# A two-layer hybrid decoder step: gate projections dealt out between the convolutions, squares and convolution states on ScalarE, second weight parts on VectorE

## Chip, cores and metric

One core of one Trainium2 chip runs the whole program. The metric is the device time of one execution in microseconds (us), as the median of several runs. The engines are named as the profile names them: PE is TensorE's matmul, PEld its weight load, DVE VectorE, ACT ScalarE, POOL GpSimd, SP SyncE (which here only issues transfers).

## What is computed

Each of two layers takes 320 tokens (256 of a prompt, 8 x 8 of samples) through one wide input projection and three token mixers, and merges them by gates:

```python
x = x + (sum_b sigmoid(h_gate_b) * (branch_b @ w_br_b)) @ w_out     # b: pooling, latent attention, DeltaNet
xn = rmsnorm(x);  h = xn @ w_in      # 7344 columns: pooling, q, kv, z's, q/k/v of DeltaNet, gates (3 x 1024)
# DeltaNet branch: a causal convolution of width 4 on 1536 channels, silu, l2-norm of q and k,
# then a chunked delta rule (chunks of 64 tokens); the last 3 pre-convolution rows are an output
qkv = silu(y);  y[t] = sum_j xx[t + j] * w[j];  conv_state = xx[-3:]
q_d, k_d = l2norm(q), l2norm(k)
```

## The kernel before

**Projections.** Activations stand transposed: 128 channels on the partitions, 320 tokens along the row. Every 128 columns of a weight are one projection: SP loads 512 KB into one of four buffers `wraw` (L176), `split_w` makes two parts of it, `wh` by ACT (L196) and the remainder `wl = wraw - wh` (L197), and `mm3` multiplies by 24 matmuls of 320 columns (8 slices times `wh`·`xnH`, `wh`·`xnL`, `wl`·`xnH`: L220, L221, L222) into a PSUM tile. `wh` and `wl` are double buffered, as is the PSUM tile `pj`. The remainder is made by DVE, except where the number of the split within the layer stands in the list `lo` of the layer's table `KS`: there POOL makes it.

**A gate** (`gate`, L460, L461) is such a projection, an elementwise product on DVE and a tanh on ACT. Each layer has 24 of them, and they depend on nothing but the normalised input, so they can stand anywhere before the merge.

**A convolution** (`conv`, `conv_out`) is a projection, two products with `rn` into `V` (L496, L497), the state columns in and out of `V` on POOL (L498 in; L499, L500 out into `cnew`), a first tap on ACT (L503), three taps on DVE (L505), a tanh on ACT (L507) and two products on DVE (L512, L516). There are twelve a layer: four for k (`unit(0, p)`, tile `kk`), four for q (`unit(1, p)`, tile `qq`), four for v (`value`, tile `co`). For k and q a square `sq` follows on POOL (L538), a matmul that sums it (L540) and, when all four are there, a logarithm and an exponential over them (`unit_norm`, L545, L546).

**Order.** The scheduler of the framework sets each engine's order by a timeline of its own, from the order in which the code is written; every engine then runs its instructions in order. The table `KS` holds one row of numbers a layer. `fillers` is a list of closures (the remaining convolutions, pooling, late projections), in the order `fo`; `fill(n)` writes out the next n. `kk`, `ft`, `fu`, `fy`, `fz` say how many fillers go between which steps of the DeltaNet preparation and recurrence; `ga`, `gm`, `gb`, `gs` how many gates are written after the decay products, within the triangular inverse, ahead of the q products, and within the recurrence over chunks.

**Stages of a layer.** The convolution stage ends with the first matmul `Y` (L793): it holds the convolutions, the decay products `D`, `AT` and the 8 x 8 inverse `R` (L756 to L768), a chain of small DVE steps. After it come the rest of the triangular inverse, the chunk products, the recurrence (L1041 `ws`, L1048 `us`, L1056 the new state) and the attention queries, then attention, then the merge.

Of the kernel before, what the change touches and what calls it, by code (L numbers as in the profile page):

```python
# [14 lines left out]
AF = mybir.ActivationFunctionType  # L15
# [22 lines left out]
WARM, WN, TA = 8, 6, 1  # L38
XK, XL, XD = 2, 2, (0, 2, 4)

KS = [{'kk': [1, 1, 2, 3], 'ga': 3, 'gm': [0, 2, 0], 'un': 16, 'gb': 0, 'gc': [0, 0, 0], 'ft': [5, 2, 3, 3, 2], 'fu': [0, 1, 2, 1], 'fn': 3, 'gs': [0, 0, 2, 1, 0], 'gq': 0, 'gp': [0, 0, 0, 0, 0, 1, 1, 0], 'ge': [1, 1, 1], 'ya': 'B', 'zb': 'A', 'fy': [2, 1, 1], 'fz': [1, 1, 1], 'p1': [2, 2, 2, 2], 'p2': [2, 2, 2, 2], 'hd': [3, 0, 2, 1, 1, 1, 0, 0], 'fo': [0, 1, 2, 3, 4, 5, 6, 7, 8, 9, 12, 13, 10, 14, 11, 18, 15, 16, 17, 19], 'to': [0, 2, 6, 1, 3, 5, 7, 13, 14, 8, 15, 16, 18, 9, 17, 10, 4, 11, 12], 'bt': ['A', 'A', 'A', 'A', 'M'], 'lo': [1, 2, 4, 5, 8, 13], 'zp': [-1, -1, -1, 19, -1, -1, -1, -1], 'f8': 3}, {'kk': [1, 1, 2, 3], 'ga': 3, 'gm': [0, 0, 0], 'un': 8, 'gb': 1, 'gc': [0, 0, 0], 'ft': [5, 2, 3, 3, 1], 'fu': [0, 1, 2, 1], 'fn': 3, 'gs': [0, 0, 2, 1, 0], 'gq': 0, 'gp': [0, 0, 0, 0, 0, 1, 1, 0], 'ge': [1, 1, 2], 'ya': 'B', 'zb': 'B', 'fy': [2, 1, 2], 'fz': [1, 0, 1], 'p1': [2, 2, 3, 1], 'p2': [2, 2, 2, 2], 'hd': [3, 0, 2, 1, 1, 1, 0, 0], 'fo': [0, 1, 5, 2, 3, 4, 6, 7, 8, 9, 12, 13, 10, 14, 11, 18, 15, 16, 17, 19], 'to': [0, 2, 5, 1, 6, 3, 7, 13, 14, 8, 15, 16, 18, 9, 17, 10, 4, 11, 12], 'bt': ['A', 'A', 'A', 'M', 'M'], 'lo': [1, 2, 4, 5, 15], 'zp': [-1, -1, -1, 19, -1, -1, -1, -1], 'f8': 3}]
LEVELS = (8, 16, 32)

GP, GL, SPILL = (1, 5), (2, 2, 2, 2, 2, 2, 1, 1), 14
# [72 lines left out]
def trunk(tc, I, O, layers=2):  # L117
    nc = tc.nc
    ctx = ExitStack()
    mult, add, sub, amax, amin = ALU.mult, ALU.add, ALU.subtract, ALU.max, ALU.min  # L120
# [18 lines left out]
    def ps(tag, name):  # L139
        return banks["pool"].tile([128, 512], F32, tag=tag, name=name, bufs=banks["n"][tag])  # L140
# [23 lines left out]
    act = nc.scalar.activation  # L164
# [182 lines left out]
    for t, (x, n) in enumerate(xnat):  # L347
        sq = pt.tile([128, 4 * T], F32, tag="l2", name="sq", bufs=2)[:, :DM]
# [19 lines left out]
    for k in range(8):  # L368
        b = ps(tags[k % len(tags)], "xt")
# [14 lines left out]
    b = ps(RNB, "rn")  # L384
# [25 lines left out]
    for l in range(layers):  # L410
        turn[0], K = 0, KS[l]
        P = prm[l]
# [62 lines left out]
        b = ps(STB, "stT")  # L475
# [6 lines left out]
        cnew = pt.tile([128, 12, 32], F32, name="cnew")  # L482
# [3 lines left out]
        b = ps("A", "spT")  # L486
# [80 lines left out]
        i = act(SM[32:40, :], SM[32:40, :], AF.Exp, scale=-1.0)  # L567
# [12 lines left out]
        gc = SM[64:72, :]  # L580
# [13 lines left out]
        b = ps("M", "tok")  # L594
# [8 lines left out]
        b = ps("M", "el")  # L603
# [77 lines left out]
        fillers = [lambda p=p: unit(1, p) for p in range(4)]  # L681
# [99 lines left out]
        for m in LEVELS:  # L781
            last = m == LEVELS[-1]
            Ys = []
            for t in range(2):
# [10 lines left out]
                for hi in second if last else (slice(0, 128),):  # L795
                    i = act(Yb[hi], Y[hi], AF.Copy)
# [4 lines left out]
            for t in range(2):  # L801
# [11 lines left out]
                else:  # L813
                    o = first(TS_[:, 0], m)
# [15 lines left out]
        for q in range(3):  # L830
            b = ps("pj", "cn")
# [38 lines left out]
        p2 = p2c.enter_context(tc.tile_pool(name=f"p2_{l}", bufs=1, side="right", reuse_waits="tile"))  # L870
# [213 lines left out]
        sq = kv5[:, :, 0]  # L1084
# [7 lines left out]
        for p in range(4):  # L1092
            b = ps("A", "oT")
# [15 lines left out]
        for p in range(4):  # L1109
            b = ps("A", "kn")  # L1110
# [222 lines left out]
        with tc.manual_schedule(engines={mybir.EngineType.PE, mybir.EngineType.DVE, mybir.EngineType.Activation, mybir.EngineType.Pool}):  # L1333
# [9 lines left out]
            for t in range(2):  # L1343
                b = ps("A", "vv")
# [7 lines left out]
            for h in range(11):  # L1352
# [10 lines left out]
                if h in GP:  # L1363
                    b = gate_mm("A", w)
# [12 lines left out]
            gs = [gate_w() for _ in range(GL[0])]  # L1377
# [3 lines left out]
            o = None  # L1381
            for bb in range(NB):
# [18 lines left out]
                if two:  # L1401
                    b = gate_mm("A", gs[1][1], ks=(0, 4))
# [25 lines left out]
        b = ps("A", "oml")  # L1428
# [33 lines left out]
        for mp in range(4):  # L1462
            for i in range(2):
                m = 2 * mp + i
                w = split_w(load_w(I["w_out"][l][:, m * 128 : m * 128 + 128], 8, 128), 8)
                b = ps("pj", "wo")
# [3 lines left out]
                if not last:  # L1470
                    i = split_x(xn[0][:, m, :], xn[1][:, m, :], xT[:, m, :], scale=prm[l + 1][:, m : m + 1])
# [57 lines left out]
```

## Time and profile before

| | before |
|---|---|
| median of 3 runs | 1063.83 us (1061.71 to 1064.25) |
| the profiled execution's own time | 1066.27 us |
| its span in the trace | 1064.5 us |
| PE busy in the span | 995.7 us (94%) |
| DVE busy | 725.8 us (68%) |
| ACT busy | 456.5 us (43%) |
| POOL busy | 338.0 us (32%) |

The difference of 1.8 us between the execution's time and the span is what lies around the first and the last profiled instruction. Busy shares are means over stages; the rows below are by stage.

### The profile page before, as it was taken

Reading aid. Unit: us, or ns where it says so; the run is one execution under the profiler, and the core shown is the slowest. Engines: PE = TensorE matmul, PEld = TensorE weight load, DVE = VectorE, ACT = ScalarE, POOL = GpSimd, SP = SyncE. Lnnn points to the kernel's source line nnn. Section 1 sums busy time; section 2 is a strip of 40 time slices with the busy share of each in tenths; the row PEclk is TensorE's granted clock in tenths of the full one; section 3 lists DMA queues with packets and bytes.
Section 4 is the critical chain, followed back from the end, with each engine's and each line's share of the span. In section 5 each row is a group of like instructions: output and inputs, shape, how many; then the busy total and the mean of one; then the engine's idle time right before and its main releaser. Section 6 shows DMA issues by size and latency. Waiting matters only on the chain.

```text
span 1064.5 us, 24733 instructions
## 1 busy us (share of the span) xinstructions
PE 995.7 (94%) x10179; PEld 866.4 (81%) x10179; DVE 725.8 (68%) x1387; ACT 456.5 (43%) x810; POOL 338.0 (32%) x469
## 2 busy tenths in 40 slices
PE   8988899999979999989989979999998899999996
PEld 6877798987857888779978868999876678777996
DVE  3999884558676666558748988656666657574872
ACT  5663353543433333334545624336344333334453
POOL 3666221215151101025445542211335211100641
PEclk8999899999989999999998989999998899999998
DMA  8532333733645776258663332355255376742961
GB/s 231 155 97 80 100 92 84 206 95 106 190 139 158 237 242 222 96 154 233 158 200 79 101 99 70 101 153 141 71 162 182 102 254 211 248 157 83 278 169 50
DMA packets 202697, 159.22 MB, mean 150 GB/s; under 512 B 27704, under 2 KB 191826, under 8 KB 200010
## 3 DMA queue, kind: packets, MB, share of 16 engines
q1 hardware_dynamic: 176364, 98.47, 34.1%
q0 software_dynamic: 7424, 48.75, 13.0%
q10 hardware_dynamic: 18798, 10.44, 3.4%
q8 instruction: 80, 1.31, 0.5%
q14 instruction: 31, 0.25, 0.1%
HBM read 144.17 MB, written 13.68 MB: 148 GB/s over the span
## 4 chain that ended last, share of the span: by engine, by line
PE 71%; DVE 15%; ACT 5%; issue 3%; DMA 3%; POOL 1%; ACTq 0%; SPq 0%; DVEq 0%; POOLq 0%
PE sc L1166 6%; PE pv L1237 5%; PE gate L220 5%; PE pj L220 5%; PE pj L222 5%; PE gate L222 4%; PE pj L221 4%; PE gate L221 4%; DVE cy L505 4%; PE br L220 3%; PE br L221 2%; DVE wl L197 2%; PE br L222 2%; PE wo L220 2%; PE wo L222 2%
## 5 line engine op out<-in xcount | busy, mean ns | idle before, releaser
L196 ACT ACTIVATE wh<-wraw 128x1024 fp32r<-128x1024 f32 (+1 forms) x180 | 166.4, 935 | 174.3 <-PE pj L221 93.0
L197 DVE TENSOR_TENSOR wl<-wraw,wh 128x1024 fp32r<-128x1024 f32 (+2 forms) x165 | 187.9, 1147 | 69.2 <-ACT wh L196 68.2
L220 PE MATMUL pj<-xnH,wh 128*128 128x320 f32 (+1 forms) x528 | 174.7, 331 | 13.5 <-DVE V L497 7.6
L222 PE MATMUL pj<-xnH,wl 128*128 128x320 f32 (+1 forms) x528 | 172.3, 326 | 6.7 <-DVE wl L197 6.4
L221 PE MATMUL pj<-xnL,wh 128*128 128x320 f32 (+1 forms) x528 | 170.0, 322 | 0.0
L220 PE MATMUL gate<-xnH,wh 128*128 128x320 f32 x384 | 124.7, 325 | 1.5 <-DVE V L497 1.5
L222 PE MATMUL gate<-xnH,wl 128*128 128x320 f32 x384 | 120.5, 314 | 1.8 <-DVE wl L197 1.3
L220 PEld LDWEIGHTS pj<-xnH,wh 128*128 128x128 f32 (+1 forms) x528 | 103.4, 196 | 21.1 <-ACT wh L196 6.9
L221 PE MATMUL gate<-xnL,wh 128*128 128x320 f32 x384 | 119.4, 311 | 0.0
L222 PEld LDWEIGHTS pj<-xnH,wl 128*128 128x128 f32 (+1 forms) x528 | 103.1, 195 | 11.6 <-DVE wl L197 7.8
L221 PEld LDWEIGHTS pj<-xnL,wh 128*128 128x128 f32 (+1 forms) x528 | 103.3, 196 | 3.2 <-issue 1.8
L220 PEld LDWEIGHTS gate<-xnH,wh 128*128 128x128 f32 x384 | 72.8, 190 | 9.6 <-issue 6.3
L1156 DVE STREAM_TRANSPOSE KT<-kv 128x1024 f32<-128x1024 f32 x64 | 78.6, 1228 | 0.6
L222 PEld LDWEIGHTS gate<-xnH,wl 128*128 128x128 f32 x384 | 72.7, 189 | 3.3 <-DVE wl L197 1.8
L221 PEld LDWEIGHTS gate<-xnL,wh 128*128 128x128 f32 x384 | 72.8, 190 | 1.1 <-issue 0.8
L220 PE MATMUL br<-yH,wh 128*128 128x320 f32 x192 | 60.3, 317 | 5.7 <-ACT wh L196 1.9
L1237 PE MATMUL pv<-kv,PT 128*64 128x256 f32 x512 | 58.8, 382 | 2.3 <-ACT PT L1215 2.3
L1166 PE MATMUL sc<-KT,q 32*64 32x256 f32 x2048 | 59.9, 380 | 0.0
L221 PE MATMUL br<-yL,wh 128*128 128x320 f32 x192 | 59.6, 313 | 0.0
L222 PE MATMUL br<-yH,wl 128*128 128x320 f32 x192 | 59.1, 313 | 0.0
L505 DVE SCALAR_TENSOR_TENSOR cy<-V,prm,cy 128x344 f32<-128x344 f32 x72 | 56.5, 804 | 0.5
L1166 PEld LDWEIGHTS sc<-KT,q 32*64 32x64 f32 x2048 | 45.8, 132 | 12.7 <-issue 6.2
(406 smaller groups left out, 2055.2 us busy)
## 6 DMA issues: line engine op xcount, KB each, us to landing
wraw<-in_w_in SPq DMA_DIRECT2D x114, 512.0 KB
wraw<-in_w_out SPq DMA_DIRECT2D x16, 512.0 KB
q<-q4d SPq DMA_DIRECT2D x64, 72.0 KB
gate<-gt ACTq DMA_DIRECT2D x28, 160.0 KB
gt<-gate POOLq DMA_DIRECT2D x28, 160.0 KB, 3.6
wraw<-in_w_br_pool SPq DMA_DIRECT2D x16, 256.0 KB
wraw<-in_w_br_dn SPq DMA_DIRECT2D x16, 256.0 KB
wraw<-in_w_br_mla SPq DMA_DIRECT2D x16, 256.0 KB
```

What stands on the lines that cost most here:

```text
L196: act(h, raw, AF.Copy)
L197: (nc.gpsimd.tensor_tensor if spare or turn[0] in K["lo"] else tt)(lo, raw, h.bitcast(F32), sub)
L220: nc.tensor.matmul(out, wh[:, k, :], xh[:, first + k, :], start=k == 0, stop=False)
L221: nc.tensor.matmul(out, wh[:, k, :], xl[:, first + k, :], start=False, stop=False)
L222: nc.tensor.matmul(out, wl[:, k, :], xh[:, first + k, :], start=False, stop=k == nk - 1)
L505: stt(y, V[:, j : j + 344], wj(j), y, mult, add)
L1156: nc.vector.transpose(v[:, a], kv[:, a * 1024 : a * 1024 + 1024].rearrange("p (i k c) -> p i k c", i=4, k=8))
L1166: nc.tensor.matmul(sc[64 * hf : 64 * hf + 64, g, :256], q4[r, k, :], krT[r, keys_] if k == 8 else KT[r, k, keys_], start=k == 0, stop=k == 8,)
L1237: nc.tensor.matmul(pv[64 * hf : 64 * hf + 64, :256], PT[:, n * 128 + 64 * hf : n * 128 + 64 * hf + 64], kv[:, r : r + 256], start=n == 0, ...
```

## The change

Four edits, the first three in the code:

- Twelve times a layer, the two copies on POOL into `cnew` (L499, L500) become one on ACT: the last three columns of the prompt and of each of eight samples stand 11 apart in `V`, so one pattern of 9 x 3 reads all 27.
- The eight squares a layer (L538) go from POOL to ACT.
- `g0` writes one gate ahead of each of the third and fourth k convolution, and the value -1 in `fo` stands for a gate among the fillers: three of them, between the first four q and v convolutions. `kk` grows from 7 fillers to 10, which takes in those three.
- In the tables: `lo` is emptied (six POOL remainders in layer 0, five in layer 1 go to DVE). The five gates a layer are taken from elsewhere: `ga` from 3 to 1 in both layers, `gm` from 2 to 1 in layer 0, `gb` from 1 to 0 in layer 1, and `gs` from 3 to 1 in both. The number of gates written before attention stays 8 and 7.

```diff
-            nc.gpsimd.tensor_copy(cnew[:, ct, 0:3], V[:, 256:259])
-            nc.gpsimd.tensor_copy(cnew[:, ct, 3:27].rearrange("p (b j) -> p b j", j=3), Vs[:, :, 8:])
+
+            last3 = bass.AP(V.tensor, V[:, 256:].offset, [V.ap[0], [11, 9], [1, 3]])
+            act(cnew[:, ct, 0:27].rearrange("p (b j) -> p b j", j=3), last3, AF.Copy)
...
-            nc.gpsimd.tensor_tensor(sq, o, o, mult)
+            act(sq, o, AF.Square)
...
+        for _ in range(K["g0"][0]):
+            gate("pj")
         unit(0, 2)
+        for _ in range(K["g0"][1]):
+            gate("pj")
         unit(0, 3)
...
-        fillers = [fillers[i] for i in K["fo"]]
+
+        fillers = [fillers[i] if i >= 0 else lambda: gate(chunk.get("tag", "pj")) for i in K["fo"]]
```

The changed kernel's lines behind these places are numbered 1 (from `act(cnew...)`, L501) to 6 higher. Three places in the engines' orders:

VectorE in layer 0, from the second convolution's `V` on, before (`cy` are the taps, `kk` a finished k convolution, `kr`, `SM` and `al` the small columns of the projection):

```order
L496 TENSOR_TENSOR V<-pj,rn 128x256
L497 TENSOR_TENSOR V<-pj,rn 128x8x8
L505 SCALAR_TENSOR_TENSOR cy<-V,prm_197,cy 128x344 x6
L512 SCALAR_TENSOR_TENSOR kk<-ct,cy 128x256
L516 SCALAR_TENSOR_TENSOR kk<-ct,cy 128x64
L562 TENSOR_TENSOR kr_397<-pj,rn 32x320
L566 TENSOR_TENSOR SM<-pj,rn 8x320
L573 TENSOR_TENSOR al<-pj,rn 8x320
```

The same place now:

```order
L496 TENSOR_TENSOR V<-pj,rn 128x256
L497 TENSOR_TENSOR V<-pj,rn 128x8x8
L197 TENSOR_TENSOR wl<-wraw,wh 128x1024
L506 SCALAR_TENSOR_TENSOR cy<-V,prm_197,cy 128x344 x5
L563 TENSOR_TENSOR kr_395<-pj,rn 32x320
L567 TENSOR_TENSOR SM<-pj,rn 8x320
L506 SCALAR_TENSOR_TENSOR cy<-V,prm_197,cy 128x344
L197 TENSOR_TENSOR wl<-wraw,wh 128x1024
L513 SCALAR_TENSOR_TENSOR kk<-ct,cy 128x256
L517 SCALAR_TENSOR_TENSOR kk<-ct,cy 128x64
```

Two remainders now stand among the taps; before, POOL made them.

ScalarE in layer 0, a little later, before (`l` copies the summed squares out of PSUM, `ct` is the tanh):

```order
L507 ACTIVATE ct<-cy 128x344
L567 ACTIVATE SM<-SM 8x320
L570 DMA xs_218<-xT 128x2560
L196 ACTIVATE wh<-wraw 128x1024
L576 ACTIVATE t_406<-t_406 8x320
```

The same place now:

```order
L508 ACTIVATE ct<-cy 128x344
L196 ACTIVATE wh<-wraw 128x1024
L539 ACTIVATE sq<-kk 128x320 x2
L461 ACTIVATE gt<-gt 128x320
L542 ACTIVATE l_264<-l_311 128x320
L577 ACTIVATE t_404<-t_404 8x320
L578 ACT_TABLE_LOAD
L578 ACTIVATE t_404<-t_404,epsc 8x320
L542 ACTIVATE l_264<-l_360 128x320
L196 ACTIVATE wh<-wraw 128x1024
```

The squares and the gate's tanh stand ahead of the next `wh`, and wait there for DVE. As many ACT_TABLE_LOAD stand in the whole order as before, 29.

TensorE in layer 0's recurrence, ahead of the `ws` of the fourth chunk, before; 37 gate matmuls stand between the products `op` of the chunk before it and this `ws`, and these are the last of them:

```order
L222 MATMUL gate<-xnH,wl 128x320
L220 MATMUL gate<-xnH,wh 128x320
L221 MATMUL gate<-xnL,wh 128x320
L222 MATMUL gate<-xnH,wl 128x320
L1041 MATMUL ws<-s,WT 64x64 x8
L1054 MATMUL qs<-s,qq 64x64 x8
```

The same place now, with 13 gate matmuls and one of the query projection `uq` in between:

```order
L222 MATMUL gate<-xnH,wl 128x320
L220 MATMUL uq<-cqH,wh 128x320
L1047 MATMUL ws<-s,WT 64x64 x4
L914 MATMUL wukT<-cst,wuk 128x128 x4
L1047 MATMUL ws<-s,WT 64x64 x4
L1060 MATMUL qs<-s,qq 64x64 x8
```

In all, 72 gate matmuls (three gates) more stand ahead of the first `Y` of each layer, and 72 fewer behind it.

## Rows read from the trace of the kernel before

**Rows 1.** Windows: both convolution stages, what follows each, and a piece of the merge.

```profile
core 0: us, PE busy (x) PEld busy (x) DVE busy (x) ACT busy (x) POOL busy (x), PEclk, DMA share, GB/s
28.00:123.70 95.70, 83.11 (x546) 74.42 (x544) 88.24 (x171) 45.73 (x72) 54.08 (x82) 0.93 0.40 109
123.70:290.00 166.30, 163.28 (x1937) 143.49 (x1937) 108.19 (x201) 73.81 (x117) 45.95 (x54) 1.00 0.46 126
545.00:645.00 100.00, 84.44 (x561) 76.16 (x559) 84.46 (x169) 48.30 (x73) 50.51 (x82) 0.91 0.38 103
645.00:810.00 165.00, 162.94 (x1925) 143.81 (x1926) 106.54 (x201) 71.96 (x118) 44.40 (x54) 0.99 0.45 127
490.00:520.00 30.00, 30.00 (x207) 30.00 (x206) 23.96 (x35) 15.25 (x24) 11.32 (x10) 1.00 0.76 218
```

**Rows 2.** Waits of PE in layer 0's convolution stage: total, times, longest.

```profile
PE pj L220 <- DVE V L497: 2.8, 1, 2.8
PE pj L222 <- DVE wl L197: 2.5, 3, 1.5
...
PE pj L220 <- ACT wh L196: 1.0, 1, 1.0
```

**Rows 3.** Longest pieces of layer 0's chain, 28 to 124 us: start, us.

```profile
29.24 2.34 DVE cy L505
...
49.86 2.33 DVE cy L505
83.91 2.32 DVE co L516
```

**Rows 4.** Timeline of POOL in the same stage: start, us, what.

```profile
37.05 0.90 POOL L538 TENSOR_TENSOR sq<-kk 128x320 f32<-128x320 f32 x1
...
49.41 2.39 POOL L197 TENSOR_TENSOR wl<-wraw,wh 128x1024 fp32r<-128x1024 f32 x1
...
83.59 2.56 POOL L197 TENSOR_TENSOR wl<-wraw,wh 128x1024 fp32r<-128x1024 f32 x1
```

**Rows 5.** Timeline of DVE in the same stage: start, us, what.

```profile
36.17 1.20 DVE L512 SCALAR_TENSOR_TENSOR kk<-ct,cy 128x256 f32<-128x256 f32 x1
37.30 0.74 DVE L516 SCALAR_TENSOR_TENSOR kk<-ct,cy 128x64 f32<-128x64 f32 x1
...
59.51 1.21 DVE L197 TENSOR_TENSOR wl<-wraw,wh 128x1024 fp32r<-128x1024 f32 x1
...
73.89 0.42 DVE L512 SCALAR_TENSOR_TENSOR qq<-ct,cy 128x256 f32<-128x256 f32 x1
74.22 0.22 DVE L516 SCALAR_TENSOR_TENSOR qq<-ct,cy 128x64 f32<-128x64 f32 x1
...
74.83 0.86 DVE L505 SCALAR_TENSOR_TENSOR cy<-V,prm,cy 128x344 f32<-128x344 f32 x1
...
95.36 0.48 DVE L460 TENSOR_TENSOR gt<-gate,rn 128x320 f32<-128x320 f32 x1
95.76 0.57 DVE L505 SCALAR_TENSOR_TENSOR cy<-V,prm,cy 128x344 f32<-128x344 f32 x1
```

**Rows 6.** Groups of POOL by form, 28 to 123.7 us: busy, mean ns, idle before.

```profile
L197 POOL TENSOR_TENSOR wl<-wraw,wh 128x1024 fp32r<-128x1024 f32 x4 | 9.7, 2431 | 0.1
L499 POOL COPY cnew<-V 128x3 f32<-128x3 f32 x12 | 5.9, 488 | 11.6 <-DVE V L496 11.5
```

**Rows 7.** The first of these in layer 1, 545 to 645 us.

```profile
L197 POOL TENSOR_TENSOR wl<-wraw,wh 128x1024 fp32r<-128x1024 f32 x3 | 7.3, 2447 | 2.5 <-ACT wh L196 2.5
```

**Rows 8.** Groups of ACT by form: a square, whole run; a small copy, first 145 us.

```profile
L399 ACT ACTIVATE sq<-hq 128x320 f32<-128x320 f32 x6 | 2.8, 468 | 2.6 <-POOL sq L401 1.9 <-DVE hq L698 0.6
...
L586 ACT ACTIVATE EG<-SM 8x8 f32<-8x8 f32 x1 | 0.2, 199 | 0.0
```

**Rows 9.** The longest wait of ACT in layer 0's convolution stage.

```profile
ACT ct L507 <- DVE cy L505: 17.8, 7, 3.7
```

**Rows 10.** Timeline: one step of layer 0's recurrence, `us`, new state, next `ws`.

```profile
214.78 0.68 PE L1048 MATMUL us<-ktv 64*64 64x64 f32 x16
...
217.51 0.41 DVE L1056 TENSOR_TENSOR s<-s,us 128x256 f32<-128x256 f32 x1
...
218.73 0.68 PE L1041 MATMUL ws<-s,WT 64*64 64x64 f32 x16
```

More of the change, by code (lines that the diff above doesn't have):

```diff
@@ L39 @@
 XK, XL, XD = 2, 2, (0, 2, 4)
-KS = [{'kk': [1, 1, 2, 3], 'ga': 3, 'gm': [0, 2, 0], 'un': 16, 'gb': 0, 'gc': [0, 0, 0], 'ft': [5, 2, 3, 3, 2], 'fu': [0, 1, 2, 1], 'fn': 3, 'gs': [0, 0, 2, 1, 0], 'gq': 0, 'gp': [0, 0, 0, 0, 0, 1, 1, 0], 'ge': [1, 1, 1], 'ya': 'B', 'zb': 'A', 'fy': [2, 1, 1], 'fz': [1, 1, 1], 'p1': [2, 2, 2, 2], 'p2': [2, 2, 2, 2], 'hd': [3, 0, 2, 1, 1, 1, 0, 0], 'fo': [0, 1, 2, 3, 4, 5, 6, 7, 8, 9, 12, 13, 10, 14, 11, 18, 15, 16, 17, 19], 'to': [0, 2, 6, 1, 3, 5, 7, 13, 14, 8, 15, 16, 18, 9, 17, 10, 4, 11, 12], 'bt': ['A', 'A', 'A', 'A', 'M'], 'lo': [1, 2, 4, 5, 8, 13], 'zp': [-1, -1, -1, 19, -1, -1, -1, -1], 'f8': 3}, {'kk': [1, 1, 2, 3], 'ga': 3, 'gm': [0, 0, 0], 'un': 8, 'gb': 1, 'gc': [0, 0, 0], 'ft': [5, 2, 3, 3, 1], 'fu': [0, 1, 2, 1], 'fn': 3, 'gs': [0, 0, 2, 1, 0], 'gq': 0, 'gp': [0, 0, 0, 0, 0, 1, 1, 0], 'ge': [1, 1, 2], 'ya': 'B', 'zb': 'B', 'fy': [2, 1, 2], 'fz': [1, 0, 1], 'p1': [2, 2, 3, 1], 'p2': [2, 2, 2, 2], 'hd': [3, 0, 2, 1, 1, 1, 0, 0], 'fo': [0, 1, 5, 2, 3, 4, 6, 7, 8, 9, 12, 13, 10, 14, 11, 18, 15, 16, 17, 19], 'to': [0, 2, 5, 1, 6, 3, 7, 13, 14, 8, 15, 16, 18, 9, 17, 10, 4, 11, 12], 'bt': ['A', 'A', 'A', 'M', 'M'], 'lo': [1, 2, 4, 5, 15], 'zp': [-1, -1, -1, 19, -1, -1, -1, -1], 'f8': 3}]
@@ new lines @@
+KS = [{'kk': [2, 1, 3, 4], 'ga': 1, 'gm': [0, 1, 0], 'g0': [1, 1], 'un': 16, 'gb': 0, 'gc': [0, 0, 0], 'ft': [5, 2, 3, 3, 2], 'fu': [0, 1, 2, 1], 'fn': 3, 'gs': [0, 0, 1, 0, 0], 'gq': 0, 'gp': [0, 0, 0, 0, 0, 1, 1, 0], 'ge': [1, 1, 1], 'ya': 'B', 'zb': 'A', 'fy': [2, 1, 1], 'fz': [1, 1, 1], 'p1': [2, 2, 2, 2], 'p2': [2, 2, 2, 2], 'hd': [3, 0, 2, 1, 1, 1, 0, 0], 'fo': [0, -1, 1, 2, -1, 3, 4, -1, 5, 6, 7, 8, 9, 12, 13, 10, 14, 11, 18, 15, 16, 17, 19], 'to': [0, 2, 6, 1, 3, 5, 7, 13, 14, 8, 15, 16, 18, 9, 17, 10, 4, 11, 12], 'bt': ['A', 'A', 'A', 'A', 'M'], 'lo': [], 'zp': [-1, -1, -1, 22, -1, -1, -1, -1], 'f8': 3}, {'kk': [2, 1, 3, 4], 'ga': 1, 'gm': [0, 0, 0], 'g0': [1, 1], 'un': 8, 'gb': 0, 'gc': [0, 0, 0], 'ft': [5, 2, 3, 3, 1], 'fu': [0, 1, 2, 1], 'fn': 3, 'gs': [0, 0, 1, 0, 0], 'gq': 0, 'gp': [0, 0, 0, 0, 0, 1, 1, 0], 'ge': [1, 1, 2], 'ya': 'B', 'zb': 'B', 'fy': [2, 1, 2], 'fz': [1, 0, 1], 'p1': [2, 2, 3, 1], 'p2': [2, 2, 2, 2], 'hd': [3, 0, 2, 1, 1, 1, 0, 0], 'fo': [0, -1, 1, 5, 2, -1, 3, -1, 4, 6, 7, 8, 9, 12, 13, 10, 14, 11, 18, 15, 16, 17, 19], 'to': [0, 2, 5, 1, 6, 3, 7, 13, 14, 8, 15, 16, 18, 9, 17, 10, 4, 11, 12], 'bt': ['A', 'A', 'A', 'M', 'M'], 'lo': [], 'zp': [-1, -1, -1, 22, -1, -1, -1, -1], 'f8': 3}]
```

## The prediction, made before the changed kernel ran

> **What bounds it now.** I first cut each layer at its first `Y` matmul and read the windows [rows 1]. Behind that point PE is the bound: busy 163.3 of 166.3 us in layer 0 and 162.9 of 165.0 in layer 1, at a granted clock of 1.00 and 0.99, with DVE at 65%. There a matmul less is time less. The convolution stage is different: DVE is busy 88.2 of 95.7 us and 84.5 of 100.0, PE only 83.1 and 84.4, at clocks of 0.93 and 0.91. So PE loses 12.6 and 15.6 us to waits in the two stages, and some 7% and 9% of the rest to the lower clock. Next I asked PE's waits who ends them [rows 2]: in layer 0 the longest two are for DVE, `V` (2.8 us) and the remainder `wl` (2.5 us, three times); `wh` by ACT costs 1.0. The stage is DVE's, and PE has holes in it.
>
> Then: is DVE really that full? The chain's longest pieces in the stage are single taps of 2.34 and 2.33 us and one product of 2.32 us [rows 3]. A tap takes 0.57 us elsewhere, and that product's form 0.22 [rows 5]. The timeline of POOL explains them: POOL's remainders of 2.39 and 2.56 us start at 49.41 and 83.59 [rows 4], just ahead of the second and third, and DVE comes free when they end. So a DVE instruction that meets a POOL instruction on SBUF stands until POOL is done; part of DVE's 88.2 us is POOL's time.
>
> **The change, part by part.**
>
> *Gates.* Three gates a layer, 72 matmuls, leave the PE-bound part. The merge's piece has 207 matmuls of this kind in 30.00 us, 0.145 us each [rows 1]: 72 x 0.145 = 10.4 us a layer, **-20.9 us** for both, if nothing else fills their place. The two gates taken from `ga` only move within the convolution stage; I count them at nothing, since DVE's total in the stage is the same and DVE ends it.
>
> *What DVE gains in the stage.* Four POOL remainders lie in layer 0's stage [rows 6]. They held DVE by 2.34 - 0.57, 2.33 - 0.57, 2.32 - 0.22 [rows 3] and, from 36.17 us, 1.20 - 0.42 [rows 5]: 6.4 us. Three lie in layer 1's [rows 7]; at the same 1.6 us each, 4.8. Squares: POOL's at 37.05 us takes 0.90 [rows 4] and DVE's product at 37.30 takes 0.74 instead of 0.22; the last of six such meetings is the tap at 74.83, 0.86 instead of 0.57 [rows 5]. Six times between 0.5 and 0.3 make 2.3 us; the same for layer 1. The state copies cost DVE nothing that I can find: they are short, and their mean of 0.49 us [rows 6] is mostly their own waiting.
>
> *What DVE pays.* A remainder on DVE is 1.21 us, a gate's product 0.48 [rows 5]. Layer 0: 4 x 1.21 + 3 x (1.21 + 0.48) = 9.9 us; layer 1: 3 x 1.21 + 5.1 = 8.7. The other two POOL remainders of each layer lie ahead of the stage, where DVE waits for the layer's first inputs; I cost them at nothing, and at 4 x 1.21 = 4.8 us if they should stand on the path.
>
> *The balance.* DVE needs 88.2 - 6.4 - 2.3 + 9.9 = 89.4 of the present 95.7 us in layer 0, and 84.5 - 4.8 - 2.3 + 8.7 = 86.1 of 100.0 in layer 1. PE needs 83.1 + 10.4 = 93.5 and 94.8, at the present low clock. Both fit into the present length, so the lower end of the stretch is nothing. The upper end is the gates' own DVE time on top, 3 x 1.69 = 5.1 us a layer, which happens if the relief falls where DVE was not on the path. PE and DVE wait for each other through two buffers each, and with both over 90% full some of the holes will stay. I take the middle: **+5.1 us** for both layers, bounds 0 and 10.2.
>
> The Trainium skill speaks against the emptied `lo`: "Perfetto Trace Analysis", section "Optimizing Scalar/DVE Operations", says that with a saturated DVE moving work to ScalarE or even GpSimd may make sense, here the reverse is done. The same section adds that such a move between DVE and GpSimd might not help, as they share a port, and "SBUF — State Buffer", section "Who interferes with whom", says that a DVE instruction with two SBUF inputs fully blocks against a GpSimd instruction that reads SBUF. By the first half alone, the seven remainders would cost 7 x 1.21 = 8.5 us with no relief; by the lock, 8.5 less 11.2. The trace agrees with the lock: 2.33 us for a tap of 0.57.
>
> *ScalarE.* A square of this size takes ACT 0.47 us, a small copy 0.20 [rows 8]; with 8 squares, 12 copies and three gates (a `wh` and a tanh, about 1.5 us together) ACT goes from 45.7 to about 57 of 95.7 us [rows 1]. It has the room, and the order has no more table loads than before; in sum nothing. What counts is whom the squares hold up, see the rivals.
>
> *Transfers.* The gates' weights, 1.5 MB a layer, load some 100 us earlier, in a stage where the DMA engines are 40% busy [rows 1]. Hidden.
>
> *What is late next.* The gates taken from the recurrence covered its steps: from `us` over the new state to `ws` it took 214.78 to 218.73, less 0.68 for the `us` matmuls themselves, 3.3 us, of which DVE's addition is 0.41 [rows 10]. Ahead of the fourth chunk's `ws` there now stand 13 gate matmuls and one more instead of 37, 2.0 us instead of 5.4. If DVE is as late as in that row, PE waits 1.3 us; there are two such places a layer (`gs` lost two gates), so 0 to 2.6 us a layer. Where DVE is free the step is under a microsecond. I take 1.1 a layer, **+2.2 us**.
>
> **Sum.** -20.9 + 5.1 + 2.2 = -13.6 us. Against the profiled execution's 1066.27 us this is 1052.7; that execution lies 2.4 us above the median of the three runs, 1063.83, so I predict **1050 us** for the median. Its own range, with the two bounded terms at both ends: -20.9 to -8.1, that is 1043 to 1056.
>
> **Rivals.**
>
> *Squares block ScalarE's queue (the other side).* ACT runs in order, and squares and tanhs now stand ahead of the next `wh`. In layer 0's stage ACT already waited 17.8 us for DVE's taps in seven waits before the tanh, 2.5 each [rows 9]. If each of 16 squares holds a `wh` on PE's path for 1.5 us, that is 24 us: 1074. It decides from 13.6 / 16 = 0.85 us a square. Against it: `wh` cost PE only 1.0 us in the stage [rows 2], it has a spare buffer, and a square waits for a product that directly follows the tanh, which ACT waited for anyway. 10%.
>
> *DVE takes the gain.* No relief from POOL (its remaining products, which read SBUF too, now meet the added remainders instead), full price for all of the above: 9.9 + 8.7 - 20.9 + 2.2 = -0.1: 1064. For it: the inverse masks (`ATm`), decay products and state columns stay on POOL. Against: over a third of POOL's 54.1 us of work goes. 12%.
>
> *Half.* Stretch and re-opened waits at their upper ends, and the early remainders on the path: -20.9 + 10.2 + 5.2 = -5.5, and +4.8 for the remainders, so 1058 to 1063; the bulk above 1056 but clearly below before. 15%.
>
> *More.* The stage gets shorter, not longer: DVE's 89.4 us leave 6 us free, and with the gates as filler PE's clock may stay up, which gives back part of the 7% and 9%. With 3.5 us less a layer in place of 2.5 more: -20.9 - 7.0 + 2.2 = -25.7: 1038. 10%.
>
> That the change does nothing is no rival: the built order has the 72 matmuls on the other side of `Y` in both layers.
>
> **How the numbers follow.** The forecast (1043 to 1056) has 53%, the rivals 10, 12, 15 and 10%. 0.3% of the time, 3.2 us, is about what a measurement can tell from no change. Faster by more: the forecast, "more" and "half", 0.78; within: "DVE takes the gain", 0.12; slower: 0.10. The range reaches from 1042, which leaves out most of "more", to 1061, which takes in most of "half" and leaves out the upper two: about 2 in 10 outside.
>
> **What would show it.** In the changed kernel's trace: (1) no DVE tap of over 2 us in the convolution stages, DVE busy near 89 and 86 us between the same marks; (2) the stages no more than 5 us longer than 95.7 and 100.0, with PE over 90% busy; (3) from the first `Y` to the end of the query stage 9 to 10 us less in each layer, PE still over 96% busy; (4) PE's waits for `us`/`ws` under 2.6 us a layer; (5) PE's waits for `wh` still a few microseconds. I am wrong if PE's longest waits in the stage are for `wh` or for a square, or if the stage grows by what the next one loses.

## The result, and the profile after

The changed kernel takes 1069.3 us (median of 20 runs, 1066.14 to 1074.37), the kernel before 1063.93 (20 runs, 1061.36 to 1067.95). The ratio is 1.0054, with a 95% interval from 1.0042 to 1.0066: slower by 5 to 6 us, where 1050 was forecast. The profiled execution of after took 1068.79 us, with a span of 1067.0.

The windows of after answer to [rows 1], cut at its own first `Y` and at the same distance behind it.

```profile
core 0: us, PE busy (x) PEld busy (x) DVE busy (x) ACT busy (x) POOL busy (x), PEclk, DMA share, GB/s
28.00:125.90 97.90, 88.94 (x623) 81.52 (x621) 85.83 (x182) 56.69 (x98) 28.08 (x45) 0.98 0.45 123
125.90:290.00 164.10, 153.60 (x1849) 135.00 (x1849) 103.41 (x196) 66.90 (x108) 45.52 (x54) 0.96 0.43 119
545.00:647.00 102.00, 93.20 (x676) 85.15 (x674) 87.29 (x179) 57.84 (x101) 32.38 (x51) 1.00 0.46 123
647.00:812.00 165.00, 154.90 (x1841) 134.59 (x1838) 105.73 (x194) 67.85 (x112) 46.09 (x54) 0.97 0.43 121
```

The convolution stage went as forecast: DVE is busy 85.8 and 87.3 us, PE over 90%, the granted clock rose from 0.93 and 0.91 to 0.98 and 1.00. The part behind it did not. In layer 0 PE has less to do there (153.6 us instead of 163.3) and stands idle for most of the difference: 10.5 us instead of 3.0.

Cutting both layers at events instead of at fixed times shows where the 2.5 us between the two spans come from. The numbers are differences of start times in the traces: first `stT` transpose of a layer, first `Y`, first `kn`, first `psc` (the attention's first score product), then the next layer's `stT` or the end. They come from one profiled execution of each kernel, and kernels that differ only behind a stretch are up to 4 us apart in it. The last three kernels are experiments told below.

| us, layer 0 / layer 1 | stT to Y | Y to kn | kn to psc | psc to next |
|---|---|---|---|---|
| before | 105.6 / 99.1 | 158.0 / 153.8 | 7.3 / 7.3 | 257.5 / 257.9 |
| after | 107.0 / 97.1 | 157.3 / 154.3 | 13.6 / 8.8 | 252.7 / 257.2 |
| engines alone (e1) | 103.4 / 91.6 | 164.4 / 155.1 | 7.3 / 7.3 | 253.9 / 256.7 |
| after with three edits (e10) | 108.6 / 97.2 | 148.0 / 149.5 | 7.3 / 7.3 | 253.3 / 257.3 |
| engines alone with the same (e12) | 99.3 / 91.3 | 162.6 / 154.4 | 7.3 / 7.3 | 255.5 / 257.4 |

From `Y` to `kn` 20.9 us were to go; 0.2 went. From `kn` to `psc`, which the prediction did not look at, 7.9 came on top. The attention of layer 0 is 4.8 us shorter in after; the engines-alone kernel has 3.6 of these too, with no wait ahead.

Some 3 us of layer 0's 157.3 are a low clock right behind `Y`, where PE had waited 1.1 us:

```profile
130.00:135.00 5.00, 5.00 (x21) 5.00 (x20) 2.57 (x6) 0.00 (x0) 0.96 (x3) 0.50 0.40 108
```

Over the first 10 us behind `Y` the clock is 0.66 in after and 1.00 in before. It is 1.00 also in the kernels of experiment 2, of experiment 3 (two buffers alone) and of experiment 7, with the same gate places. So from `Y` to the fourth `us` layer 0 takes 111.4 us in before, 108.6 in after and 105.4 to 105.7 in those.

**Where PE stands.** Waits of PE in after, layer 0 (first from `Y` on, then 284 to 300 us), then layer 1 from 647 us: total, times, longest.

```profile
PE oT L1102 <- DVE so L995: 3.6, 1, 3.6
...
PE ws L1043 <- DVE kqs L1035: 0.6, 1, 0.6
PE oT L1102 <- DVE zs L1103: 0.5, 1, 0.5
...
PE vv L1352 <- DMA wuv<-in_w_uv: 4.3, 1, 4.3
```

```profile
PE scn L993 <- DVE so L995: 2.9, 1, 2.9
PE oT L1102 <- DVE zs L1103: 2.2, 1, 2.2
PE us L1054 <- DVE ktv L1050: 1.4, 1, 1.4
```

The waits for `us` and `ws`, on which the prediction put 1.1 us a layer, are as small as it said (0.6 and 1.4 + 0.9). The large ones stand at the end of the recurrence, at `oT` and `scn`, and at `vv`. (The wait at `oT` is put down to `so`, which runs on DVE right behind the product `ot` that `oT` reads; `ot` ends at 278.16, `oT` starts at 278.35.)

**Why `oT` is late.** ACT before, in layer 0 (start, us, what):

```profile
265.51 1.28 ACT L1088 ACT_TABLE_LOAD   x1
266.80 0.31 ACT L1088 ACTIVATE r<-r,epsc 128x20 f32<-128x20 f32 x1
267.13 1.28 ACT L1089 ACT_TABLE_LOAD   x1
...
270.63 5.18 ACTq L981 DMA_DIRECT2D q4d<-qlat  x8
```

DVE before, at the same place; the reduction of the chain had run at 264.25:

```profile
267.17 0.74 DVE L970 COPY qlat<-qlat 128x256 f32<-128x256 f32 x2
268.77 1.49 DVE L1091 TENSOR_TENSOR ot<-ot,r 128x1280 f32<-128x1280 f32 x1 [0.86 <-ACT r L1089]
```

ACT after:

```profile
266.69 5.18 ACTq L987 DMA_DIRECT2D q4d<-qlat  x8
271.97 0.47 ACT L435 ACTIVATE th<-zs 128x320 f32<-128x320 f32 x1 [9.91 <-DMA q4d<-qlat]
272.46 1.28 ACT L1094 ACT_TABLE_LOAD   x1
273.75 0.31 ACT L1094 ACTIVATE r<-r,epsc 128x20 f32<-128x20 f32 x1
273.97 1.04 ACT L196 ACTIVATE wh<-wraw 128x1024 fp32r<-128x1024 f32 x1
275.03 1.28 ACT L1095 ACT_TABLE_LOAD   x1
```

DVE after:

```profile
265.58 1.41 DVE L976 COPY qlat<-qlat 128x256 f32<-128x256 f32 x4
266.91 1.47 DVE L1093 TENSOR_REDUCE r<-ktv 128x20 f32<-128x1280 f32 x1
...
276.67 1.49 DVE L1097 TENSOR_TENSOR ot<-ot,r 128x1280 f32<-128x1280 f32 x1 [3.71 <-ACT r L1095]
```

The normalisation of DeltaNet's output is a serial chain: a reduction on DVE, two table functions on ACT (`r`), a product on DVE (`ot`), then the transposing products `oT` on PE. Before, ACT ran `r` ahead of the eight `q4d` transfers that it issues for the latent queries. After, the built order has the copies of `qlat` ahead of the reduction on DVE and the transfers ahead of `r` on ACT, 5.18 us of issuing, and `r` starts 7 us later (272.46 against 265.51). `oT` starts at 278.4 in both: before, `ot` was done 8 us earlier, and matmuls of PE filled the time but for 1.1 us; now there are fewer, and PE waits 3.6 us for the chain.

**The wait costs twice.** Windows of after around `oT`:

```profile
272.00:274.00 2.00, 2.00 (x16) 1.73 (x14) 0.49 (x1) 1.97 (x4) 0.00 (x0) 1.00 0.37 62
274.00:276.00 2.00, 0.77 (x4) 0.51 (x4) 0.00 (x0) 1.98 (x3) 0.00 (x0) 0.88 0.00 0
276.00:278.00 2.00, 0.00 (x0) 0.00 (x0) 1.33 (x1) 1.94 (x4) 0.00 (x0) 0.50 0.00 0
278.00:280.00 2.00, 1.65 (x30) 1.65 (x32) 1.77 (x7) 0.93 (x2) 0.30 (x1) 0.50 0.04 8
280.00:282.00 2.00, 1.46 (x28) 1.27 (x28) 2.00 (x4) 0.33 (x1) 1.70 (x2) 0.50 0.61 123
```

The third number from the right is the granted clock. It falls to 1.2 of 2.4 GHz in the wait and stays there when work is back, until 282.

**Why `vv` waits.** Issues of SP and POOL in after, and the same two in before:

```profile
282.15 0.37 SPq L1132 DMA_DIRECT2D wuv<-in_w_uv  x1
...
279.69 1.07 POOL L1142 DMA_INDIRECT kv<-in_cache_kv_latent,idr  x1 [14.66 <-ACT kn L1114]
```

```profile
280.51 0.37 SPq L1126 DMA_DIRECT2D wuv<-in_w_uv  x1
...
280.33 1.07 POOL L1136 DMA_INDIRECT kv<-in_cache_kv_latent,idr  x1 [16.22 <-ACT th L435]
```

Before, the load of `wuv` (512 KB) went out together with the gather of the latent cache, and `vv` began at 285.5 without a wait. After, it follows 2.5 us behind the gather and lands 9.34 us after its issue by the chain, at 291.5. SP could not issue it earlier: it waited 16.4 us for a `zs` of DVE, 12.8 before. In layer 1 of after PE has no wait for `wuv`; the 1.6 us more from `kn` to `psc` there come with a clock of 0.50 between 802 and 804 us, behind the wait of 2.2 us at `oT`, while PE is busy throughout.

### The profile page after: what moved, and what is told of

Read it like the earlier page. It is cut to its first block, busy times and chain, and to the rows that moved or that the text cites. A ratio compares the mean times of both kernels' runs of the same rounds, so it can differ in the third digit from the quotient of the medians.

```text
span 1067.0 us, 24688 instructions
## 1 busy us (share of the span) xinstructions
PE 990.0 (93%) x10179; PEld 861.0 (81%) x10179; DVE 723.7 (68%) x1398; ACT 466.1 (44%) x850; POOL 283.9 (27%) x394
## 3 DMA queue, kind: packets, MB, share of 16 engines
q0 software_dynamic: 7424, 48.75, 12.8%
## 4 chain that ended last, share of the span: by engine, by line
PE 65%; DVE 18%; ACT 6%; issue 5%; DMA 3%; ACTq 1%; POOL 1%; DVEq 0%; SPq 0%; POOLq 0%
PE sc L1172 6%; PE pv L1243 5%; PE gate L220 4%; PE pj L220 4%; PE pj L222 4%; PE pj L221 4%; DVE wl L197 4%; PE gate L222 4%; PE gate L221 4%; DVE cy L506 3%; PE br L220 3%; PE br L221 3%; PE br L222 3%; PE wo L220 2%; PE wo L222 2%
## 5 line engine op out<-in xcount | busy, mean ns | idle before, releaser
L197 DVE TENSOR_TENSOR wl<-wraw,wh 128x1024 fp32r<-128x1024 f32 (+2 forms) x176 | 203.4, 1164 | 74.1 <-ACT wh L196 73.0
L220 PE MATMUL pj<-xnH,wh 128*128 128x320 f32 (+1 forms) x528 | 171.1, 324 | 5.9 <-ACT wh L196 2.4
L221 PE MATMUL pj<-xnL,wh 128*128 128x320 f32 (+1 forms) x528 | 167.7, 318 | 0.0
L222 PEld LDWEIGHTS pj<-xnH,wl 128*128 128x128 f32 (+1 forms) x528 | 100.6, 191 | 16.6 <-DVE wl L197 12.6
L220 PEld LDWEIGHTS pj<-xnH,wh 128*128 128x128 f32 (+1 forms) x528 | 100.7, 191 | 13.1 <-issue 5.3
L221 PEld LDWEIGHTS pj<-xnL,wh 128*128 128x128 f32 (+1 forms) x528 | 100.5, 190 | 1.9 <-issue 0.4
L1202 ACT ACTIVATE S<-S,mx 128x1024 f32<-128x1024 f32 x16 | 18.4, 1151 | 86.0 <-DVE mx L1201 86.0
```

Source lines behind the costliest of these rows:

```text
L197: (nc.gpsimd.tensor_tensor if spare or turn[0] in K["lo"] else tt)(lo, raw, h.bitcast(F32), sub)
L220: nc.tensor.matmul(out, wh[:, k, :], xh[:, first + k, :], start=k == 0, stop=False)
L221: nc.tensor.matmul(out, wh[:, k, :], xl[:, first + k, :], start=False, stop=False)
L222: nc.tensor.matmul(out, wl[:, k, :], xh[:, first + k, :], start=False, stop=k == nk - 1)
L1202: act(S, S, AF.Exp, bias=mx[:, 4:5], accum_out=mx[:, 5:6])
```

## The experiments

Each ratio is against runs of the kernel before on the same chip, with its 95% interval. "After" stands at 1.0054.

**1. Engines alone, gates alone.** The first kernel has before's tables, but `lo` emptied and the new code for squares and states; the second has after's tables with `lo` and the GpSimd code of before. The first against after, part of layer 0's row:

```
-'kk': [2, 1, 3, 4], 'ga': 1, 'gm': [0, 1, 0], 'g0': [1, 1], 'gs': [0, 0, 1, 0, 0]
+'kk': [1, 1, 2, 3], 'ga': 3, 'gm': [0, 2, 0], 'g0': [0, 0], 'gs': [0, 0, 2, 1, 0]
...
```

> The changed kernel with every gate where it stood before; only the squares, the convolution states and the second weight parts are on their new engines. Theory A (behind the first Y the layer waits on a chain of latencies, so the gates there were free filler, and gates between the convolutions only lengthen that stage): the engine moves alone shorten the convolution stage by 2 to 5 us a layer and nothing is lost behind it, so 1055 to 1061 us, below both kernels. Theory B (the engine moves themselves cost, by ScalarE's queue or VectorE's longer weight work): 1066 to 1071 us, near the changed kernel. Theory C (the loss is the wuv load that now lands behind the 2 MB gather, by chance of the order of issue): 1060 to 1064 us if the gather is issued after it again, as before.

> The changed kernel's gate places with the engines of before: squares, convolution states and the listed second weight parts on GpSimd. Theory A: GpSimd and VectorE share the convolutions as before and 72 matmuls a layer come on top, with nothing won behind the first Y: 1070 to 1080 us, above both. Theory B (the engine moves cost): 1055 to 1062 us. Theory C (wuv behind the gather): 1067 to 1072 us, as the changed kernel, if the gates set the order of the two issues.

Engines alone: 1058.23 us, 0.9931 (0.9910 to 0.9953). Gates alone: 1072.97 us, 1.0075 (1.0046 to 1.0104). So the engine moves gain 6 to 7 us with the old gate places and 2 with the new (1.0075 to 1.0054), and the gates' move costs 8 us with the old engines and 13 (1.0054 less 0.9931) with the new ones. Theory B, that the engine moves cost, falls; both times lie in the ranges of theory A.

**2. `wuv` early.** The load gets a buffer of its own and is issued far ahead of the gather.

```
+wuv0 = p2.tile([128, 1024], F32, name="wuv0").rearrange("p (c n) -> p c n", c=2)
+nc.sync.dma_start(wuv0, I["w_uv"][l].rearrange("(c p) h d -> p c (h d)", p=128))
...
-wuv = load_wuv(ph.tile([128, 1024], F32, name="wuv"))
+wuv = wuv0
```

> The changed kernel with the wuv load issued at the start of the attention part's set-up into a buffer of its own, ahead of the kv gather; nothing else. Theory C (wuv behind the gather is the loss): the 4.3 us that TensorE waits at vv in layer 0 go, and what layer 1 loses there, so 1063 to 1066 us. Theory A: the wait goes but most of it comes back before layer 1 starts (4.8 us came back between psc and the states of layer 1), so 1067 to 1069 us.

1063.22 us, 0.9982 (0.9966 to 0.9998). The edit is worth 7.7 us by the ratios (1.0054 to 0.9982), in the range of theory C. From `kn` to `psc` it takes 7.3 us in both layers, instead of 13.6 and 8.8. The 6.3 us of layer 0 were this collision: the wait of 4.3 us and a clock of 0.64 and 0.50 in the 4 us behind it (292 to 296 us). The 1.6 of layer 1 were not: the kernel with both edits of experiment 3 has 9.0 us there again, with `wuv` early. Theory A, that most of it comes back before layer 1, was wrong in this.

**3. Two buffers for the `w_uq` load** (`RQ = 1` becomes 2), then both edits.

> The changed kernel with two buffers for the w_uq load, so that the second half's load need not wait until VectorE has read the first. Theory A, in the form that this load heads the chain (issued 234.0, landed 238.0, then wh, wl, kqs, ws at 244.3 in both kernels): ws comes 3 to 4 us earlier, oT and kn follow, 1061 to 1066 us. Rival: another link of the recurrence sets ws or oT: 1068 to 1070 us.

> The changed kernel with the wuv load ahead of the gather and two buffers for the w_uq load, both at once. If the two waits are separate (one at vv, one ahead of ws and oT), their gains of about 6 us each add up: 1055 to 1059 us. If they share a cause (the recurrence's tail is late and both loads wait on it), the second adds nothing: 1061 to 1064 us. In the forecast's sense, with the tail free TensorE would be the bound again and the gates' move would pay: below 1055 us.

Two buffers: 1063.53 us, 0.9989 (0.9970 to 1.0008). Both: 1057.64 us, 0.9912 (0.9880 to 0.9943), so they add: 7.7 and 6.9 us singly, 15.1 together, by the ratios. No matmul is added or taken away by either. From the fourth `us` to `oT` layer 0 takes 43.9 us in after and 42.2 with both, with 330 matmuls each time; layer 1 takes 37.9 and 33.3. In layer 1 the built order moved too: 254 matmuls stand in the stretch instead of 269, about 2.2 us by the price of 0.145, and the stretch ahead of it is 3.0 us longer. Over `Y` to `kn` both layers together are 6.9 us shorter.

**4. A gate back into the recurrence's end, in two places.** First `gs` gets the fourth chunk's gate back and a -1 goes from `fo`; then `ga`'s gate is written directly ahead of `oT`.

```
-'kk': [2, 1, 3, 4], 'gs': [0, 0, 1, 0, 0]
+'kk': [2, 1, 3, 3], 'gs': [0, 0, 1, 1, 0]
```

```
+for _ in range(K["gq"]):
+    gate("pj")
 for p in range(4):
     b = ps("A", "oT")
```

> The changed kernel with one of the three gates a layer, the one behind the fourth chunk of the recurrence, put back there and taken from the fillers between the convolutions. Theory (that stretch, from the fourth us to oT, took 43.2 and 36.8 us with the gate and 43.8 and 37.9 without it, so the gate was free filler): the convolution stage shortens by 2 to 3 us a layer, the tail takes as long as with no gate: 1062 to 1066 us. Rival (TensorE's throughput bounds the tail too, as in the prediction): 3.5 us a layer come back there, 1069 to 1072 us.

> The changed kernel with one gate a layer taken from ahead of the first Y and written directly ahead of oT, behind the sample chunk's ws, where TensorE waits 4.1 and 2.2 us for VectorE. Theory (a gate there is filler, one between the convolutions costs nearly its full 3.5 us): 1062 to 1065 us, with ws to oT still 37 and 36 us or less although 24 matmuls more stand in it. Rival (zero sum, TensorE's throughput bounds both): 1068 to 1071 us. A side effect is possible: the order of the pooling's projections around the first Y moves too.

1082.69 us, 1.0159 (1.0135 to 1.0184), and 1069.70 us, 1.0027 (1.0001 to 1.0053). The theory missed both; the first lies above either range, the second in the rival's. Yet neither settles what a gate costs there, since neither put it where PE was idle. In the first, a projection of the pooling moved ahead of layer 1's first `Y` as well, and that stage grew from 97.1 to 107.2 us; in layer 0 the gate stood ahead of the sample chunk's `ws`, which heads the chain, and the stretch to `oT` grew from 43.9 to 46.8. In the second, the gate came to stand behind the wait it was to fill. PE in layer 1:

```profile
792.04 1.12 PE L993 MATMUL scn<-hkv,qlat 128*128 128x64 f32 x4 [4.21 <-DVE so L995]
...
795.80 0.47 PE L221 MATMUL gate<-xnL,wh 128*128 128x320 f32 x1
796.06 0.47 PE L222 MATMUL gate<-xnH,wl 128*128 128x320 f32 x1
```

The gate's matmuls start 0.27 us apart here, against 0.145 in [rows 1]: the granted clock is 0.50 from 792 to 800 us, behind the wait of 4.21 us.

**5. Old gate places, new engines, both edits.**

> The first experiment's kernel (engines of the change, gates where they were) with the wuv load ahead of the gather and two buffers for w_uq. If both waits cost there too: 1046 to 1052 us. If the gates behind the first Y cover them, as filler: 1056 to 1060 us, no better than without. Against the kernel that has the same two edits and the new gate places it says whether spreading the gates is worth anything once these waits are gone.

1059.36 us, 0.9939 (0.9918 to 0.9959), no better than the engines alone (0.9931). With the gates in place the edits buy nothing.

**6. The engine moves apart.** Before with an empty `lo`; before with squares and states moved.

> The kernel before with the list of second weight parts on GpSimd emptied, nothing else. By the prediction's prices (GpSimd's remainders held VectorE for 6.4 and 4.8 us, on VectorE they cost 1.21 us each, four and three in the stages): 1060 to 1062 us, 1.5 and 1.2 us a layer less. If emptying the list is the whole gain of the engine moves: 1057 to 1060 us. If VectorE is the bound and the lock was covered: 1066 to 1070 us, and the gain came from the squares and states.

> The kernel before with only the squares and the convolution states moved to ScalarE; gates and second weight parts as before. The three engine moves together gave a ratio of 0.9931, the weight parts alone 0.998. If the parts add: 0.995, 1059 to 1061 us against 1064.5. If the gain needs all of GpSimd's work gone from the stage: 1063 to 1066 us, no change. By the prediction's price for the squares (2.3 us a layer): 1060 us. Rival (squares block ScalarE's queue): above 1066 us.

1063.92 us, 0.9980 (0.9963 to 0.9997), and 1071.46 us, 1.0029 (1.0007 to 1.0052). The parts do not add up to the 0.9931 of both: `stT` to `Y` takes 204.7 us over both layers before, 202.3 with the empty `lo`, 204.5 with squares and states moved, and 195.0 with both. The second lies in the range that its expectation gave to the rival (squares block ScalarE's queue). On its chip before took 1066.35. Its convolution stages are no longer than before's. In its profile, which at 1078.02 us is the slowest of its twelve executions, the time is lost from `Y` to `kn` (161.3 and 160.8 us against 158.0 and 153.8); the cause stays open.

**7. The chain itself.** The nine `q4d` transfers go from ACT's queue to SP's, on top of the two edits of 3; later the same without the second `w_uq` buffer.

```
-nc.scalar.dma_start(q4d[:, :, k, :], qlat[32 * (k % 4) : 32 * (k % 4) + 32, k // 4])
+nc.sync.dma_start(q4d[:, :, k, :], qlat[32 * (k % 4) : 32 * (k % 4) + 32, k // 4])
...
-nc.scalar.dma_start(q4d[:, :, 8, :], qc)
+nc.sync.dma_start(q4d[:, :, 8, :], qc)
```

> The changed kernel with wuv early and two w_uq buffers, and the nine q4d transfers issued by SyncE's queue in place of ScalarE's. If the tail is a chain through ScalarE's queue (q4d issues ahead of the two table functions r, then ot, then oT), ot comes 5 to 8 us earlier and oT 2 to 4 us a layer: 1050 to 1055 us. If TensorE or the w_uq chain sets oT by now: 1056 to 1059 us. If SyncE's queue holds the transfers up behind weight loads: above 1060 us, with the wait at the query load.

> The changed kernel with wuv early and q4d on SyncE's queue, but one w_uq buffer. With wuv alone it was 1063.2, with wuv and the second buffer 1057.6, with all three 1050.7. If the edits' parts add: 1055 to 1058 us. If the w_uq load ahead of ws then heads the chain and hides the q4d edit: 1061 to 1064 us.

1050.71 us, 0.9856 (0.9819 to 0.9892), the best of all, and 1054.74 us, 0.9903 (0.9871 to 0.9935). So moving the transfers is worth 6 us with the second buffer (0.9912 to 0.9856) and 8 without it (0.9982 to 0.9903). With all three edits, ACT and DVE in layer 0:

```profile
267.64 1.28 ACT L1097 ACT_TABLE_LOAD   x1
268.93 0.31 ACT L1097 ACTIVATE r<-r,epsc 128x20 f32<-128x20 f32 x1
```

```profile
269.28 1.49 DVE L1099 TENSOR_TENSOR ot<-ot,r 128x1280 f32<-128x1280 f32 x1 [2.26 <-ACT r L1097]
```

`ot` runs at 269.28 instead of 276.67, and PE's wait at `oT` shrinks from 3.6 + 0.5 to 0.2 + 0.9 us. "DMA: Bandwidth & Descriptors" of the Trainium skill, section "Issuing engines are not separate DMA queues", says that issuing from another engine saves only the sequencer's time, usually small beside the transfer. Here one issue takes 0.65 us of ACT (5.18 for eight), against 2.06 us that after's chain shows from the end of one issue to a landing. What costs is that eight of them stand in a row ahead of `r`, which is on the path.

**8. The same edits with the old gates.**

> The change's engines, the gates where they were before, and the three edits of the run before (wuv early, two w_uq buffers, q4d on SyncE's queue). Theory (with the gates in place TensorE is busy in the tail, so a shorter chain gives nothing): 1057 to 1060 us, as without the edits (1058.2), and the move of the gates is then worth 7 to 9 us. Rival (the three edits give any kernel the same 18 us): 1040 to 1047 us, and the gates' move is worth nothing or costs.

> The kernel before with the three edits and nothing of the change. Theory: TensorE covers the chain there, 1062 to 1066 us, no change. Rival: 1046 to 1052 us, the same 18 us less.

1056.51 us, 0.9926 (0.9898 to 0.9953), and 1061.95 us, 0.9981 (0.9958 to 1.0004). Without the edits these kernels stand at 0.9931 and 1. So the three edits are worth next to nothing where the gates are in their old places, and 0.0198, some 21 us, where they have gone. That they shift the built order in layer 1 is no rival for this: layer 0 alone, with 330 matmuls from the fourth `us` to `oT` in after and in e10, goes from 43.9 to 38.3 us there. Put the other way: moving the gates costs 13 us without the edits and gains 7 with them (0.9926 to 0.9856, intervals just apart). Windows from the first `Y` to `kn`, both layers, first with the new gate places (e10), then with the old (e12):

```profile
128.40:276.50 148.10, 144.76 (x1835) 127.89 (x1834) 100.84 (x190) 64.76 (x101) 42.18 (x52) 1.00 0.43 118
634.20:783.70 149.50, 145.53 (x1809) 128.05 (x1809) 97.15 (x185) 63.44 (x99) 43.09 (x52) 0.98 0.43 118
```

```profile
118.80:281.40 162.60, 157.45 (x1904) 139.59 (x1903) 103.74 (x194) 68.51 (x106) 41.58 (x51) 0.98 0.42 114
635.50:789.90 154.40, 151.76 (x1882) 135.11 (x1881) 102.02 (x191) 67.98 (x105) 42.31 (x52) 1.00 0.45 122
```

Now matmuls that leave are time that leaves, though not at the full price: 14.6 and 4.8 us less, 19.4 in all, of which about 6 in layer 0 are an extra wait and low clock near 200 us in the old-gate kernel (see the end). Without these it is some 13 of the 20.9 us of the prediction; against before with the three edits (157.3 and 152.6 us) it is 12.3. In the convolution stage the gates cost 15.2 us (205.8 against 190.6). So most of the 7 us that the move gains here is that extra wait; what it would be worth against an old-gate kernel without the wait is not shown.

## Why the prediction was wrong

**The step that failed** is the first: "Behind that point PE is the bound ... There a matmul less is time less", and with it the term of -20.9 us. For it stood PE's busy share of 98%. But the end of that part is set by a chain through DVE, ACT, a load and ACT's transfer queue, and matmuls without dependencies filled the time beside it. The term came out at 0.2 us. The busy share cannot tell the two cases apart. From the fourth `us` to `oT` the matmuls and times were 351 in 43.3 us and 305 in 36.8 before, 330 in 43.9 and 269 in 37.9 after: fewer matmuls, no less time. With the three edits the same two stretches took 38.3 us (330 matmuls) and 31.1 (254) with the new gate places, and 42.2 and 37.0 with the old. From `Y` to the fourth `us` the step did better. In layer 0 two gates left it, worth 7.0 us by the prediction's price, and gave 2.8, or 5.8 in the kernels without the low clock behind `Y`. In layer 1 all three gates left it, worth 10.4; 38 other matmuls came in from behind, and 3.2 us were gained.

**A term that was missing**: the order of `wuv` and the gather. "Transfers ... Hidden" was right of the gates' weights and was not asked of anything behind. 7.9 us from `kn` to `psc`; experiment 2 shows the cause of layer 0's 6.3.

**The convolution stage** (+5.1, bounds 0 to 10.2) measured -0.6 over both layers from `stT` to `Y`. It is the sum of two larger parts that the prediction mixed: the engine moves give 9.7 us (204.7 to 195.0), the gates take 9.1. A moved gate costs 1.5 us of its 3.5 there (9.1 over six gates), and 2.5 in the pair of experiments 7 and 8 (205.8 against 190.6). So the gain of the engines went into paying for the gates, and the gates' own gain had to come from behind `Y`, where it did not. That the measured sum lies just under the term's lower bound, and not far outside, is luck.

**Re-opened waits in the recurrence** (+2.2): right in size, 0.6 and 2.3 us. What came on top of them stood further down the same chain. The prediction's own range counts this term's upper bound once for both layers; with 2.6 us in each its upper end is -5.5 and not -8.1, so 1058 and not 1056. The result lies outside either way.

**DVE's relief**: no tap is over 2 us; the longest are of 1.61, still against 0.57, beside the work that stays on POOL. "SBUF — State Buffer" of the Trainium skill, section "Who interferes with whom", has the rule that the prediction drew on, that a DVE instruction with two SBUF inputs and a reading GpSimd block each other. The taps agree with it: those of 2.3 us went with POOL's remainders. DVE's busy time came out at 85.8 and 87.3 us, near the 89.4 and 86.1 of the balance. With an empty `lo` and three gates more, DVE spends 8.0 us more on `wl` in layer 0 and 6.8 in layer 1, which the relief outweighs. The worth of the empty `lo` alone, 0.9980, 2.1 us, agrees with the 2.7 that follow from the prediction's prices.

Of the list of what would show it, (1), (2), (4) and (5) came as written: between the fixed marks the stages grew by 2.2 and 2.0 us (from `stT` to `Y` by 1.4 and -1.9), PE is 91% busy there, and `wh` costs PE 1.3 and 1.0 us. (3) failed, and decided it; neither of the two signs of being wrong appeared (in the stages PE waits longest in total for `wl`, 3.6 and 4.9 us). **Squares block ScalarE's queue** did not happen in after: PE's waits for a square are 1.4 us in layer 0 and 1.5 in layer 1, and engines alone gain. With squares and states moved alone they are 3.0 us in layer 0. The side on which it ended was none of the rivals: slower, by a wait behind the stretch from which the work was taken.

## What to carry to other kernels

A busy TensorE is the bound only if what keeps it busy is on the path. Before work without dependencies is taken from a stretch, follow the dependent chain through the other engines from the stretch's first step to its last, and cost what remains without the filler. Shorten that chain first: the chain's three edits gave 21 us here where the filler was gone and next to nothing where it was left. Then set what the work costs in its new place (15.2 us here) against what it frees (some 13). And look one stage further, at the order of loads that the moved work used to hold apart.

## What was not expected of the hardware

A wait of TensorE can cost again behind it. In the engines-alone kernel PE waits 2.8 us for `ss` in layer 0, near 200 us, and the granted clock is 0.50 for the work that follows:

```profile
199.00:202.30 3.30, 0.48 (x4) 0.22 (x2) 2.15 (x6) 2.05 (x5) 0.86 (x1) 0.89 1.19 330
202.30:204.00 1.70, 1.68 (x4) 0.79 (x4) 1.70 (x3) 1.68 (x3) 0.00 (x0) 0.50 0.37 84
204.00:206.00 2.00, 2.00 (x14) 1.47 (x13) 0.99 (x1) 1.97 (x4) 0.00 (x0) 0.50 0.68 157
206.00:208.00 2.00, 2.00 (x9) 2.00 (x9) 0.27 (x1) 1.68 (x2) 0.87 (x1) 0.50 1.11 303
208.00:210.00 2.00, 2.00 (x14) 2.00 (x13) 0.74 (x2) 0.00 (x0) 0.00 (x0) 0.91 0.22 64
```

Some 6 us at half the clock, about 3 us of work, as much again as the wait: its stretch from the first to the fourth `us` took 50.2 us, in before 44.2. So filler that looks worthless can be worth the clock it holds up.

The wait itself leads to ACT's transfers once more. The squares that `ss` sums stand on ACT behind four issues of the load of the states (`st`), which take 7.9 us here and 3.3 in before. In all three kernels with the new engines and the old gates these issues take 7.5 to 7.9 us, PE waits 2.4 to 2.8 us for `ss`, and the stretch takes 48.6 to 50.3 us. No run moved this load, so its part is not tested.
